# Stationary weight tiles of a hybrid decoder block: two K tiles laid out column by column in turn

## The chip, the cores and the metric

The kernel runs on one core of one Trainium2 chip. The metric is device time in microseconds (us) of one execution, as the median of several runs. A NeuronCore has five engines with instruction lists of their own: TensorE (PE in the profile; PEld is its loading of stationary weights, LDWEIGHTS), VectorE (DVE), ScalarE (ACT), GpSimd (POOL) and SyncE (SP, which here only issues DMAs). A matmul on TensorE holds a stationary block of 128 x 128 values in the array and streams a moving operand of up to 512 columns past it. Each matmul of this kernel has its own weight load.

## The reference, cut to what matters

One decoder layer over 256 tokens of width 2048, in fp32: a combined input projection, gated linear attention (GLA) and forgetting attention (FoX), a merge of the two with gates, an output projection and a layer norm, a gated MLP of width 5632 with a causal convolution on its gate path, a second layer norm, and a per-layer embedding. The parts that the change touches are plain matrix products of the token matrix with weights:

```python
proj = x @ w_in                                   # fq, fk, gq, gk are columns of it, 1024 each
...
g = causal_dwconv(x @ w_gate, conv_w, conv_b)     # x: (256, 2048), w_gate, w_up: (2048, 5632)
h = jax.nn.gelu(g) * (x @ w_up)
return h @ w_down
```

## The kernel before

Each fp32 matrix is split into a high part, rounded to the TensorE format fp32r, and a low part, the rest, and a product is built from high x high, high x low and low x high. A token tile holds, for one K tile of 128 rows, 256 columns of the high part of the activations and then 256 of the low part (`a[:, kt % 4, :]`, 512 columns).

The weights come from HBM as "units" of 128 partitions x 2048 fp32 values, 284 in all, in the order of use. `prep` fetches a unit as two halves of 1024 columns (`raw`), lets ScalarE round each into a tile `hi`, and VectorE subtract that into a tile `lo`; these tiles sit in rings of six. `unit()` hands out the next one and keeps three units ahead prepared. The order of the instructions on each engine follows the program and Tile's scheduler; SP issues its DMAs in program order.

Units are used in two ways. In most stages the activations are stationary and the weights stream past them (`x_mm`, `q_unit`: lines 353, 841, 979). In the stages that need their result with channels on partitions the weights are stationary: the FoX and GLA queries and keys (PSUM tiles psfq, psfk, psq, psk, 32 units) and the gate and up projections of the MLP (psg, psu, 88 units). There a unit is 128 output channels: 16 K tiles of 128 x 128 side by side, the first eight in `hi[0]` and `lo[0]`, the others in `hi[1]` and `lo[1]`. `w_unit` runs, for each K tile, one matmul of 512 columns with the block of `hi` (line 307) and one of 256 columns with the block of `lo` (line 309), all into one PSUM bank. `w_phase` does the same for the first three units of the MLP, in two phases by token half (lines 322 and 326, 256 columns each), while the layer norm before it still finishes. `comb` then adds the two halves of the bank. `_wst` lays the weights out on the host, before the launch.

Two other places are used for comparison in what follows: lines 713 to 718, in the GLA blocks, where levels 1 to 7 work on runs of 1, 2, 4 ... 64 words out of 2, 4, 8 ... 128; and plain fp32 matmuls (lines 628, 630, 735), which TensorE runs in two passes.

Of the kernel before, what the change touches and what calls it, by code (L numbers as in the profile page):

```python
# [19 lines left out]
P = 128  # L20
# [58 lines left out]
def tile_block(ctx: ExitStack, tc: tile.TileContext, wu, wfv, wpp, xT_in, x_in, pT_in, wlr,  # L79
               chan, gnorm, lng, ident_in, mask_in, cmask_in, out):  # L80
    nc = tc.nc
# [32 lines left out]
    def mmtile(name):  # L114
        return pmm.tile([P, 512], F32, tag="mm", name=name)
# [133 lines left out]
    def unit(ahead=3):  # L249
        u = n_used[0]  # L250
        n_used[0] += 1
        while n_prep[0] < min(NU, u + ahead):
            prep()
        return ready.pop(u)
# [42 lines left out]
            nc.gpsimd.tensor_copy(mask[:, 4 * i:4 * i + 4, :], maskf)  # L297


    def w_unit(ps, hi, lo, act, kts, first, last, hoff=0, tick=None):  # L300


        n = len(kts)
        for i, kt in enumerate(kts):
            a = act[kt // 4]
            w0 = (hoff + i) * P
            nc.tensor.matmul(ps, lhsT=hi[i // 8 if hoff == 0 else 0][:, w0 % 1024:w0 % 1024 + P],  # L307
                             rhs=a[:, kt % 4, :], start=first and i == 0, stop=False)
            nc.tensor.matmul(ps[:, 256:512],  # L309
                             lhsT=lo[i // 8 if hoff == 0 else 0][:, w0 % 1024:w0 % 1024 + P],  # L310
                             rhs=a[:, kt % 4, 0:256], start=False, stop=last and i == n - 1)
            if tick is not None:
                tick(i)

    def w_phase(ps, hi, lo, act, t, kts, part=slice(None)):


        p4 = ps.rearrange("p (s t n) -> p s t n", s=2, t=2)
        for kt in kts[part]:
            a = act[kt // 4][:, kt % 4, :]  # L320
            w = slice(kt % 8 * P, kt % 8 * P + P)
            nc.tensor.matmul(p4[:, :, t, :], lhsT=hi[kt // 8][:, w],
                             rhs=a.rearrange("p (s t n) -> p s t n", s=2, t=2)[:, :, t, :],
                             start=t == 0 and kt == kts[0], stop=False)
            if t == 1:
                nc.tensor.matmul(ps[:, 256:512], lhsT=lo[kt // 8][:, w], rhs=a[:, 0:256],
                                 start=False, stop=kt == kts[-1])

    def comb(ps, o, scale=1.0):
# [28 lines left out]
    def pull(n, gens=mixers):  # L358
        for _ in range(n):
            while gens:  # L360
                try:
                    next(gens[0])
                    break
                except StopIteration:
                    gens.pop(0)
# [92 lines left out]
    for u in range(8):  # L458
        hi, lo = fvu[u]
        for j in range(2):  # L460
            kt = 2 * u + j
            a = xT[kt // 4][:, kt % 4, :]
# [6 lines left out]
            for t, i, c in seq:  # L469
                o, n = fch[c]  # L470
                w, x = prods[t][i]
                nc.tensor.matmul(fbk[t][c][:, 0:n], lhsT=x, rhs=w[:, o:o + n],  # L472
                                 start=kt == 0 and i == 0, stop=kt == 15 and i == 2)
# [32 lines left out]
    for t in range(2):  # L506
        for c, (o, n) in enumerate(fch):
            n = min(n, 1024 - o)
# [143 lines left out]
    for n in range(16):  # L652
        h, j = n // 2, n % 2
        hi, lo = unit()

        ps = (mxtile if n == 0 else mmtile)(f"psf{'qk'[j]}{h}")
        w_unit(ps, hi, lo, xT, range(16), True, True,
               tick=lambda i: pull(1) if i == 7 else None)
        if n % 8 == 0:
            fqk[h // 4] = s8([P, 4, 2, 256], name=f"fqk{h // 4}")  # L660
        comb(ps, fqk[h // 4][:, h % 4, j], (P ** -0.5, 1.0)[j])
        if n >= 1:
            pull(1, parks)
# [105 lines left out]
    for n in range(16):  # L769
        nm, dst, sc = (("q", gq, 1.0 / 16.0), ("k", gk, 1.0))[n // 2 % 2]  # L770
        h, c = n // 4, n % 2
        hi, lo = unit()
        ps = mmtile(f"ps{nm}{2 * h + c}")
        w_unit(ps, hi, lo, xT, range(16), True, True,
               tick=lambda i: pull(1, mixers if n < 4 else levels) if i == 7 else None)
        comb(ps, dst[:, h, :].rearrange("p (t c n) -> p t c n", t=2, c=2)[:, :, c, :], sc)
        if n >= 4:
            pull(1)
        if n >= 1:
            pull(1, parks)  # L780
# [10 lines left out]
    def s_sums(y):  # L791

        a11, a21, a12, a22 = [y[:, k, t * P:t * P + P] for k in range(2) for t in range(2)]
        v = t2("sums").rearrange("p (i t) -> p i t", t=P)
        for i, a, b, op in ((0, a21, a22, ALU.add), (2, a21, a11, ALU.subtract),
                            (1, v[:, 0], a11, ALU.subtract), (3, a12, v[:, 1], ALU.subtract)):
            nc.vector.tensor_tensor(v[:, i], a, b, op)
        return v
# [328 lines left out]
    for n in range(PSM1, 32):  # L1127
        if n in (26, 28):
            i = n // 2 - 13
# [189 lines left out]
    pq, first = [], []  # L1319

    def end1(tail_mm):
# [4 lines left out]
        with tc.manual_schedule(engines={mybir.EngineType.PE}):  # L1326
# [16 lines left out]
            def phase0(i, part):  # L1343
                if i == len(us):
                    us.append(unit())
                    ps.append(mmtile(("psg0", "psu0", "psg1")[i]))
                w_phase(ps[i], *us[i], x1T, 0, kts, part)

            def phase1(j):
                for i in range(3):  # L1350
                    w_phase(ps[i], *us[i], x1T, 1, kts, slice(4 * j, 4 * j + 4))
# [60 lines left out]
    def gate_up(name):  # L1412
        if first:
            return first.pop(0)
        hi, lo = unit()
        ps = mmtile(name)
        w_unit(ps, hi, lo, x1T, range(16), True, True)
        return ps

    for n in range(NF):  # L1420
# [20 lines left out]
        pair, j = n // 2, n % 2  # L1441
# [12 lines left out]
        if pair in DN_S[0] and j == 1:  # L1454
            v = s_sums(yp)
            for i in range(2):
                w = sm.tile([P, 2, 256], F32R, tag="t2", bufs=6, name="hs")
# [3 lines left out]
                k = DN_S[0].index(pair)  # L1461
# [193 lines left out]
def _wst(w):  # L1655

    k, n = w.shape
    kt, nt = k // P, n // P
    per = 2048 // (kt * P)
    a = w.reshape(kt, P, nt // per, per, P).transpose(2, 1, 3, 0, 4)  # L1660
    return a.reshape(nt // per, P, 2048)


def _xst(w):
# [36 lines left out]
def _layout(i):  # L1701
    w_in = i["w_in"][0]
    c = lambda nm, n: w_in[:, OFF[nm]:OFF[nm] + n]
    bg, bf = _qst(i["w_branch_gla"][0]), _qst(i["w_branch_fox"][0])
    br = [w for q in range(4) for w in (bg[4 * q:4 * q + 4], bf[2 * q:2 * q + 2])]
    gu = np.stack([_wst(i["w_gate"][0]), _wst(i["w_up"][0])], 1).reshape(2 * NF, P, 2048)
    qk = np.stack([_wst(c(n, 1024)).reshape(4, 2, P, 2048) for n in ("gq", "gk")], 1)
    m = np.concatenate([_qst(c(n, 2048)) for n in ("ma", "mb")], 0)
    wu = np.concatenate(
        [np.stack([_wst(c("fq", 1024)), _wst(c("fk", 1024))], 1).reshape(16, P, 2048), qk.reshape(16, P, 2048), m[:PSM1],  # L1710
         _sst(c("gv", 2048), GV_ORDER, GV_S), _sst(c("gr", 2048), GV_ORDER, GR_S), m[PSM1:]] + br
        + [_sst(i["w_out"][0], OUT_ORDER, WO_S), gu,
# [45 lines left out]
```

## Time and profile before

| | |
|---|---|
| median of 3 runs | 1645.58 us (1645.08 to 1645.61) |
| span of the profiled execution, first to last instruction | 1645.0 us |
| TensorE matmuls, weight loads | 8422 each |
| busy: TensorE, weight loads, VectorE, ScalarE | 1638.4, 1404.3, 1356.0, 910.3 us |
| granted TensorE clock | 1.000 of full speed |
| read from HBM, written | 417.53 MB, 58.73 MB |

A row of the groups by line has the line, the engine, the operation, the tiles written and read, the shape and the count, then the busy time in us and the mean ns of one, then the idle time ahead of it and what ended it. A row of the timeline has the start in us, the duration in us, and the operation; "x2" at its end means that two like instructions in a row are merged, and the duration runs from the first's start to the last's end. Intervals of matmuls overlap, so the distance between two starts, not the duration, is what one matmul costs.

### The profile page before, as it was taken

To read this page: it belongs to the slowest core of one execution; us is meant where nothing else is said; L and a number is where in the kernel's file an instruction comes from. 1 tells how busy PE (TensorE), PEld (TensorE's weight loads), DVE (VectorE), ACT (ScalarE), POOL (GpSimd) and SP (SyncE) were. 2 spreads that over 40 slices of the span, in tenths; PEclk is the share of its full clock that TensorE was granted. 3 is DMA by queue.
4 is the path that set the end of the run, shared out by engine and by line. 5 is a ranking of instruction groups with operands and counts; after the bars stand their busy time and mean duration, and the time that the engine had idled before them with its cause. 6 is when DMAs were issued, how large, how long until landed. Compare 5 with 4: busy or idle time off the path is not lost.

```text
span 1645.0 us, 23490 instructions
## 1 busy us (share of the span) xinstructions
PE 1638.4 (100%) x8422; PEld 1404.3 (85%) x8422; DVE 1356.0 (82%) x1964; ACT 910.3 (55%) x1277; POOL 92.7 (6%) x244
## 2 busy tenths in 40 slices
PE   9999999999999999999999999999999999999998
PEld 9988888888888888887898888888888888888887
DVE  7687899788989867778987888887887778988887
ACT  6655555456666654446574445555455456566554
POOL 0000000000000000000010111110111000000000
PEclk9999999999999999999999999999999999999999
DMA  8799799878888768889855898888766679899574
GB/s 324 281 371 341 290 383 356 294 258 309 306 333 307 252 207 303 305 335 364 296 190 194 315 338 320 308 306 304 279 239 217 210 260 336 305 343 348 177 258 157
DMA packets 114838, 477.81 MB, mean 290 GB/s; under 512 B 13032, under 2 KB 14320, under 8 KB 95136
## 3 DMA queue, kind: packets, MB, share of 16 engines
q1 hardware_dynamic: 105216, 417.57, 70.8%
q0 software_dynamic: 9504, 58.73, 8.9%
q8 instruction: 66, 1.08, 0.2%
q14 instruction: 52, 0.43, 0.1%
HBM read 417.53 MB, written 58.73 MB: 290 GB/s over the span
## 4 chain that ended last, share of the span: by engine, by line
PE 97%; DMA 1%; DVE 1%; ACT 0%; issue 0%; POOL 0%; ACTq 0%
PE psm L979 11%; PE dn L841 10%; PE psu L307 10%; PE psg L307 9%; PE psa L979 5%; PE psu L309 5%; PE psg L309 5%; PE dn_p L841 4%; PE gr L841 3%; PE gv L841 3%; PE fv L472 3%; PE pg L353 3%; PE psb L979 3%; PE wo L841 2%; PE gr_p L841 2%; PE gv_p L841 2%
## 5 line engine op out<-in xcount | busy, mean ns | idle before, releaser
L241 DVE TENSOR_TENSOR lo<-raw,hi 128x1024 fp32r<-128x1024 f32 x456 | 551.1, 1220 | 140.7 <-ACT hi L121 139.4
L121 ACT ACTIVATE hi<-raw 128x1024 fp32r<-128x1024 f32 x456 | 476.6, 1057 | 304.2 <-DMA raw<-in_wu_dram 83.7
L307 PE MATMUL psu<-x1T,hi 128*128 128x512 f32 x688 | 240.4, 392 | 0.0
L307 PE MATMUL psg<-x1T,hi 128*128 128x512 f32 x672 | 234.8, 392 | 0.0
L309 PE MATMUL psu<-x1T,lo 128*128 128x256 f32 x688 | 192.3, 280 | 0.0
L309 PE MATMUL psg<-x1T,lo 128*128 128x256 f32 x672 | 187.8, 280 | 0.0
L979 PE MATMUL psm<-hi,xT 128*128 128x512 f32 x512 | 163.0, 392 | 0.0
L307 PEld LDWEIGHTS psu<-x1T,hi 128*128 128x128 f32 x688 | 129.2, 188 | 27.6
L307 PEld LDWEIGHTS psg<-x1T,hi 128*128 128x128 f32 x672 | 126.2, 188 | 27.0
L309 PEld LDWEIGHTS psu<-x1T,lo 128*128 128x128 f32 x688 | 130.6, 190 | 0.0
L121 ACT ACTIVATE hi_b<-raw 128x512 fp32r<-128x512 f32 x112 | 92.9, 841 | 66.8 <-DMA raw<-in_wu_dram 17.9
L309 PEld LDWEIGHTS psg<-x1T,lo 128*128 128x128 f32 x672 | 127.6, 190 | 0.0
L159 DVE TENSOR_TENSOR td<-td 128x512 f32<-128x512 f32 x172 | 117.6, 684 | 0.9
L215 DVE TENSOR_TENSOR lo_b<-raw,hi_b 128x512 fp32r<-128x512 f32 x112 | 104.9, 952 | 15.9 <-ACT hi_b L121 15.6
L979 PEld LDWEIGHTS psm<-hi,xT 128*128 128x128 f32 x512 | 96.2, 188 | 19.6
L215 DVE TENSOR_TENSOR lo_t<-td,hi_t 128x1024 fp32r<-128x1024 f32 x86 | 101.7, 1219 | 12.7 <-ACT hi_t L121 12.0
L121 ACT ACTIVATE hi_t<-td 128x1024 fp32r<-128x1024 f32 x86 | 88.0, 1053 | 28.9 <-DMA td<-td 15.1
L979 PE MATMUL psm<-lo,xT 128*128 128x512 f32 x256 | 99.8, 390 | 0.0
L841 PE MATMUL dn<-hi,hC 128*128 128x512 f32 x352 | 97.8, 389 | 0.0
L979 PE MATMUL psa<-hi,oT 128*128 128x512 f32 x256 | 81.2, 392 | 0.0
L841 PEld LDWEIGHTS dn<-hi,hC 128*128 128x128 f32 x352 | 66.0, 188 | 13.7
L979 PEld LDWEIGHTS psa<-hi,oT 128*128 128x128 f32 x256 | 48.1, 188 | 10.0
(414 smaller groups left out, 3130.8 us busy)
## 6 DMA issues: line engine op xcount, KB each, us to landing
raw<-in_wu_dram SPq DMA_DIRECT2D x525, 512.0 KB, 6.3
td<-in_wu_dram SPq DMA_DIRECT2D x43, 1024.0 KB, 8.8
td<-td POOLq DMA_DIRECT2D x43, 1024.0 KB, 7.7
td<-td SPq DMA_DIRECT2D x43, 1024.0 KB, 8.3
hS<-sd SPq DMA_DIRECT2D x11, 1024.0 KB, 8.8
raw<-in_wu_dram SPq DMA_DIRECT2D x43, 256.0 KB, 7.7
fvraw<-in_wfv_dram SPq DMA_DIRECT2D x13, 524.0 KB, 6.6
sd<-hs POOLq DMA_DIRECT2D x24, 256.0 KB, 5.6
```

The source lines that it names most:

```text
L121: return nc.scalar.activation(o, i, AF.Copy, bias=0.0, scale=scale)
L159: sub = lambda o, a, b: nc.vector.tensor_tensor(o, a, b, ALU.subtract)
L215: nc.vector.tensor_tensor(lo, src, hi.bitcast(F32), ALU.subtract)
L241: i = nc.vector.tensor_tensor(lo, raw, hi.bitcast(F32), ALU.subtract)
L307: nc.tensor.matmul(ps, lhsT=hi[i // 8 if hoff == 0 else 0][:, w0 % 1024:w0 % 1024 + P], rhs=a[:, kt % 4, :], start=first and i == 0, stop= ...
L309: nc.tensor.matmul(ps[:, 256:512], lhsT=lo[i // 8 if hoff == 0 else 0][:, w0 % 1024:w0 % 1024 + P], rhs=a[:, kt % 4, 0:256], start=False, ...
L353: nc.tensor.matmul(bs[j][:, 0:m], lhsT=x, rhs=v[:, o:o + m], start=first and i == 0, stop=last and i == 2)
L472: nc.tensor.matmul(fbk[t][c][:, 0:n], lhsT=x, rhs=w[:, o:o + n], start=kt == 0 and i == 0, stop=kt == 15 and i == 2)
L841: nc.tensor.matmul(ps[:, e], lhsT=x, rhs=w, start=k == 1, stop=k == total.get(id(ps), 3 * ns))
L979: nc.tensor.matmul(ps[t], lhsT=x, rhs=v, start=first and i == 0 and j == 0, stop=last and i == 3 and j == 2)
```

## The change

`_wst` interleaves pairs of K tiles: where column n of K tile 2m stood beside column n + 1 of the same tile, it now stands beside column n of K tile 2m + 1. A unit keeps its size and its place; a half of 1024 columns still holds eight K tiles, now as four pairs of 256 columns. The new function `wcols` takes the block of one K tile out of that: 128 columns with a step of two elements (8 bytes), spread over 1024 bytes, where it was 128 columns side by side. `w_unit` and `w_phase` read their stationary blocks through it, `hi` and `lo` alike. The parameter `hoff`, which no caller set, is gone. The moving operands, the PSUM tiles, the DMAs, the rounding and the subtraction stay as they are. The lists of instructions on TensorE, VectorE, ScalarE, GpSimd and SP are the same before and after, row for row.

```diff
+    def wcols(w, kt):
+
+        v = w[kt // 8].rearrange("p (k n j) -> p k j n", n=P, j=2)
+        return v[:, kt % 8 // 2, kt % 2, :]
+
-    def w_unit(ps, hi, lo, act, kts, first, last, hoff=0, tick=None):
+    def w_unit(ps, hi, lo, act, kts, first, last, tick=None):
...
-            w0 = (hoff + i) * P
-            nc.tensor.matmul(ps, lhsT=hi[i // 8 if hoff == 0 else 0][:, w0 % 1024:w0 % 1024 + P],
-                             rhs=a[:, kt % 4, :], start=first and i == 0, stop=False)
-            nc.tensor.matmul(ps[:, 256:512],
-                             lhsT=lo[i // 8 if hoff == 0 else 0][:, w0 % 1024:w0 % 1024 + P],
-                             rhs=a[:, kt % 4, 0:256], start=False, stop=last and i == n - 1)
+            nc.tensor.matmul(ps, lhsT=wcols(hi, i), rhs=a[:, kt % 4, :],
+                             start=first and i == 0, stop=False)
+            nc.tensor.matmul(ps[:, 256:512], lhsT=wcols(lo, i), rhs=a[:, kt % 4, 0:256],
+                             start=False, stop=last and i == n - 1)
...
-            w = slice(kt % 8 * P, kt % 8 * P + P)
-            nc.tensor.matmul(p4[:, :, t, :], lhsT=hi[kt // 8][:, w],
+            nc.tensor.matmul(p4[:, :, t, :], lhsT=wcols(hi, kt),
...
-                nc.tensor.matmul(ps[:, 256:512], lhsT=lo[kt // 8][:, w], rhs=a[:, 0:256],
+                nc.tensor.matmul(ps[:, 256:512], lhsT=wcols(lo, kt), rhs=a[:, 0:256],
...
 def _wst(w):
...
-    kt, nt = k // P, n // P
-    per = 2048 // (kt * P)
-    a = w.reshape(kt, P, nt // per, per, P).transpose(2, 1, 3, 0, 4)
-    return a.reshape(nt // per, P, 2048)
+    a = w.reshape(k // 256, 2, P, n // P, P).transpose(3, 2, 0, 4, 1)
+    return a.reshape(n // P, P, k)
```

## The prediction

> **What bounds the kernel now.** I read the page first: the busy times, the granted clock and the chain of work that ended last.
>
> ```profile
> span 1645.0 us, 23490 instructions
> PE 1638.4 (100%) x8422; PEld 1404.3 (85%) x8422; DVE 1356.0 (82%) x1964; ACT 910.3 (55%) x1277; POOL 92.7 (6%) x244
> PEclk9999999999999999999999999999999999999999
> PE 97%; DMA 1%; DVE 1%; ACT 0%; issue 0%; POOL 0%; ACTq 0%
> ```
>
> TensorE carries 97% of the chain at full granted clock in every slice. A busy TensorE is not a proof, since its intervals overlap, so I asked the view of waits for everything that TensorE waited for.
>
> ```profile
> PE warm_ps L131 <- DVE warm L128: 1.2, 1, 1.2
> PE wo L841 <- DVE lo_b L215: 0.4, 1, 0.4
> PE wo_p L841 <- ACT hi_t L121: 0.2, 1, 0.2
> ```
>
> That is 1.8 us in all. The time is therefore the sum of the steps from the start of one matmul to the start of the next, and a nanosecond more or less in a step is paid once per step. The profiled span of 1645.0 us lies 0.6 us under the median of the runs, 1645.58, whose spread is 0.5 us; I work on the span and give the result as if it were the median. About 0.2% (3.3 us) is what a measurement of this kernel can tell from no change.
>
> **Which steps the edit touches.** The groups by line give the number of matmuls whose stationary block is a weight tile, that is all of `w_unit` (lines 307 and 309) and `w_phase` (322 and 326).
>
> ```profile
> L309 PE MATMUL psu<-x1T,lo 128*128 128x256 f32 x688 | 192.3, 280 | 0.0
> L309 PE MATMUL psg<-x1T,lo 128*128 128x256 f32 x672 | 187.8, 280 | 0.0
> L309 PE MATMUL psfq<-xT,lo 128*128 128x256 f32 x128 | 35.9, 280 | 0.0
> L309 PE MATMUL psk<-xT,lo 128*128 128x256 f32 x128 | 35.8, 280 | 0.0
> L309 PE MATMUL psfk<-xT,lo 128*128 128x256 f32 x128 | 35.8, 280 | 0.0
> L309 PE MATMUL psq<-xT,lo 128*128 128x256 f32 x128 | 35.8, 280 | 0.0
> L322 PE MATMUL psg<-x1T,hi 128*128 128x256 f32 x64 | 12.6, 287 | 0.0
> L322 PE MATMUL psu<-x1T,hi 128*128 128x256 f32 x32 | 6.3, 284 | 0.0
> L326 PE MATMUL psg<-x1T,lo 128*128 128x256 f32 x32 | 7.9, 282 | 0.0
> L326 PE MATMUL psu<-x1T,lo 128*128 128x256 f32 x16 | 4.0, 282 | 0.0
> ```
>
> Line 309 runs 688 + 672 + 4 x 128 = 1872 times, and line 307 as often, since the loop issues one of each per K tile. Lines 322 and 326 add 144. So 3888 of the 8422 weight loads change their access pattern. 1872 matmuls are 512 wide; 1872 + 144 = 2016 are 256 wide. The timeline shows how the two widths alternate inside one unit:
>
> ```profile
> 899.74 0.39 PE L307 MATMUL psg<-x1T,hi 128*128 128x512 f32 x1
> 899.97 0.28 PE L309 MATMUL psg<-x1T,lo 128*128 128x256 f32 x1
> 900.09 0.39 PE L307 MATMUL psg<-x1T,hi 128*128 128x512 f32 x1
> ...
> 904.59 0.39 PE L307 MATMUL psg<-x1T,hi 128*128 128x512 f32 x1
> 899.97 0.19 PEld L307 LDWEIGHTS psg<-x1T,hi 128*128 128x128 f32 x1
> ```
>
> Fourteen pairs lie between 899.74 and 904.59: 4.85 / 14 = 0.3464 us a pair. The wide matmul takes 0.23 us of that, the narrow one 0.116. The last row is the point of the whole case: the weights of the next wide matmul begin to load at 899.97, when the narrow one starts, and have only its 0.116 us to hide behind.
>
> **How much room the load has.** The load's 0.19 us is a latency; its pace shows where loads follow each other.
>
> ```profile
> 209.11 0.97 PEld L735 LDWEIGHTS pa<-kq 128*128 128x128 f32 x8
> L1223 PEld LDWEIGHTS ptl<-ident,z 128*128 128x128 f32 x64 | 7.7, 140 | 1.9 <-ACT z L1216 0.5
> L307 PEld LDWEIGHTS psu<-x1T,hi 128*128 128x128 f32 x688 | 129.2, 188 | 27.6
> ```
>
> Eight loads of 128 contiguous fp32 columns take 0.97 us, so (0.97 - 0.19) / 7 = 0.111 us each. These have a 128-wide matmul each over them, so 0.111 is an upper bound of the load's own time. Against the 0.116 us of the narrow step that leaves 5 ns of cover, and against the 0.23 us of the wide step about 120 ns. The second row, the load for a transpose (mean 140 ns), takes 48 ns less than the third, a load of the edited line: the reading side can deliver the same 512 bytes faster than the usual load asks for them.
>
> **The change part by part.** No instruction is added, removed or moved; the two loops over weight tiles issue the same matmuls, with the same operands' tiles, in the same order. DMA sizes, ScalarE's rounding and VectorE's subtraction still run over whole contiguous 1024-column tiles, so they cost what they did. Unchanged terms: 0. What changes is that a load reads 128 words 8 bytes apart, over 1024 bytes, where it read 512 bytes in a run. No load of before does that, so I bound its price by other engines that read every second fp32 word. In level 1 of the GLA blocks (lines 713 to 718) ScalarE and VectorE work on 256 words with step two; in the later levels the same lines work on runs.
>
> ```profile
> 186.93 0.44 ACT L713 ACTIVATE e<-e 128x256 f32<-128x256 f32 x1 [2.33 <-DVE e L710]
> 187.26 0.43 ACT L715 ACTIVATE e<-e 128x256 f32<-128x256 f32 x1
> 194.26 0.41 ACT L713 ACTIVATE e<-e 128x256 f32<-128x256 f32 x1
> 194.57 0.41 ACT L715 ACTIVATE e<-e 128x256 f32<-128x256 f32 x1
> L718 DVE TENSOR_TENSOR kq<-gk,e x28: 408/416/426, 188.0 to 365.3; 128x256 f32<-128x256 f32 x28
> ```
>
> ScalarE takes 0.435 us at step two (first two rows, level 1 of head 0) against 0.41 at runs of 32 (level 6): 25 ns for 256 words, 0.1 ns a word. VectorE's 28 products over all seven levels lie within 408 to 426 ns: no surcharge. For a load of 128 words that makes 0 (VectorE's row) to 13 ns (ScalarE's). I take ScalarE's, because the load's pace, 128 words in at most 0.111 us, is nearer to ScalarE's than to VectorE's. The load then takes 111 + 13 = 124 ns. Under a wide matmul that stays hidden. Under a narrow one it sticks out by 124 - 116 = 8 ns, 2016 times: **16 us**. Sum: 1645.6 + 16 = **1661.6 us**.
>
> The two ends of this term. Below: if the load is at VectorE's price it stays covered, 0 us. Above: the reading could also hold up the moving stream. How much of that there is now can be bounded by plain fp32 matmuls, which take their moving columns at half the pace:
>
> ```profile
> 153.21 0.59 PE L628 MATMUL po<-pts,fv 128*128 128x256 f32 x2
> 153.64 0.38 PE L630 MATMUL po<-pts,fv 128*128 128x128 f32 x2
> ```
>
> Two passes over 256 columns start 0.43 us before the next line, 0.215 each, so half of that, 0.1075, is what 256 columns would take with nothing in the way. A pair has 768 columns: 0.3225 us against 0.3464 measured, 24 ns of surplus. If all of it came from loads crossing the moving stream, and twice the span read doubled it, the price would be 1872 x 24 ns = 45 us: 1691. It can also go the other way, below.
>
> [...]
>
> **The rivals.**
>
> *It costs nothing.* The 5 ns of cover are enough, or the load's own time lies well under 111 ns. For it: VectorE's row and the transposes' faster load. Against it: ScalarE's rows, and that the narrow step has so little room. Time: 1645.6, within 3.3 us.
>
> *It makes the steps shorter (the other sign).* Now the load advances at half the byte rate of the moving operand, so the two streams pass each other; with step two a load of 1024 bytes runs beside 256 moving words, 1024 bytes, at nearly equal pace. If the 24 ns of surplus come from the streams crossing, running in step could remove them in every pair. All of it would be 45 us, 1600; half, which I take as the price, 1623. It decides from 1.8 ns a pair (3.3 us / 1872). For it: the surplus exists, and the two streams do run side by side. Against it: nothing in the trace shows that the surplus comes from loads. What is late next would not be another engine soon:
>
> ```profile
> 900.00:1380.00 480.00, 480.00 (x2691) 421.11 (x2690) 387.10 (x602) 249.22 (x366) 50.10 (x151) 1.00 0.79 284
> ```
>
> In this stretch of the gate and up units VectorE (the third busy time) works 387 of 480 us; with 7% taken off the pairs it would be at 87%.
>
> *The load falls to half its pace.* If single words can't be read at the pace of runs, the load takes 222 ns: just hidden under the wide step, 106 ns too long under the narrow one, 2016 x 106 = 214 us: 1860. For it: no load in this trace reads with a step. Against it: neither ScalarE nor VectorE loses more than 6% at this step. [...]
>
> **How the numbers follow.** Forecast, slower by the surcharge, 1649 to 1691: 0.35, because an extra line read is likely to cost something where cover is 5 ns. Half pace: 0.16. Together slower by over 0.2%: 0.51. Nothing: 0.21. Shorter steps: 0.28. The likeliest gives 1661.6. The range leaves out half pace (0.16) and the last few us of the shorter steps: 1604 to 1691, which holds the forecast's bounds, the case of nothing and nearly all of the gain. Cases of both signs hold most of the chance; the forecast's own range is 1649 to 1691.
>
> **What would show it.** Right: the groups of lines 307 and 309 keep their counts, the loads of line 307 read some 13 ns longer than their 188, the wide step stays 0.23 and the narrow one grows from 0.116 to about 0.124, so that fourteen pairs take 4.96 us; the waits of TensorE stay near 1.8 us. Nothing: pairs stay at 0.346. Shorter steps: pairs fall toward 0.33 and both widths lose. Half pace: the narrow step is near 0.22 and the loads near 0.3. The forecast is wrong if the pair moves in its wide half, if steps of lines that are not edited (841, 979) move, or if TensorE begins to wait for weights.

## The result and the profile after

| | before | after |
|---|---|---|
| median | 1645.33 us (1644.32 to 1645.61, 4 runs) | 1657.12 us (1656.67 to 1657.49, 4 runs) |
| span of the profiled execution | 1645.0 us | 1655.2 us |

The changed kernel takes 1.0071 times as long, 95% interval 1.0056 to 1.0085: +11.8 us, 9.2 to 14.0 by the interval. The forecast was 1661.6, +16. Lines shift by two to four in the changed file: 307 and 309 are 311 and 313, 841 and 979 are 843 and 981. In the three kernels below that edit one kind of load only, 307 and 309 are 315 and 317. The page after, and its waits of TensorE:

```profile
span 1655.2 us, 23490 instructions
PE 1649.3 (100%) x8422; PEld 1419.6 (86%) x8422; DVE 1357.1 (82%) x1964; ACT 909.7 (55%) x1277; POOL 93.8 (6%) x244
PE 99%; DVE 0%; ACT 0%; POOL 0%; issue 0%; ACTq 0%
PE warm_ps L131 <- DVE warm L128: 1.2, 1, 1.2
```

Counts are as they were, VectorE and ScalarE work as long as before, TensorE waits for no other engine after the warm-up. The loss has to be inside the steps of TensorE. The groups of the page, for one of the tiles:

```profile
L311 PE MATMUL psu<-x1T,hi 128*128 128x512 f32 x688 | 245.0, 398 | 0.0
L313 PE MATMUL psu<-x1T,lo 128*128 128x256 f32 x688 | 191.3, 278 | 0.0
L981 PE MATMUL psm<-hi,xT 128*128 128x512 f32 x512 | 163.0, 392 | 0.0
L311 PEld LDWEIGHTS psu<-x1T,hi 128*128 128x128 f32 x688 | 135.5, 197 | 26.7
L313 PEld LDWEIGHTS psu<-x1T,lo 128*128 128x128 f32 x688 | 136.0, 198 | 0.0
```

Edited loads take 197 and 198 ns where they took 188 and 190. The wide matmul shows 398 where it showed 392, the narrow one 278 where it showed 280, and line 981, whose stationary operand is not edited, its 392 as before. One unit in the timeline, from its first wide matmul to that of the next unit:

```profile
1104.98 0.40 PE L311 MATMUL psg<-x1T,hi 128*128 128x512 f32 x1
1105.21 0.28 PE L313 MATMUL psg<-x1T,lo 128*128 128x256 f32 x1
...
1110.63 0.40 PE L311 MATMUL psu<-x1T,hi 128*128 128x512 f32 x1
```

Sixteen pairs in 5.65 us: 0.3531 a pair, against 0.3464 in the rows of before. Over the whole trace I summed the distances between starts: from a wide to the next narrow matmul 432.3 us before and 444.8 after (1872 of each), from a narrow one on 219.4 and 218.7, all others 987.4 and 985.8. So +12.5 - 0.7 - 1.6 = +10.2 us, the difference of the spans. The mean pair went from 0.3467 to 0.3531 us, 6.4 ns. This mean and those of pairs and steps below leave out the few steps, 10 to 20 of 3744 in each trace, that are over 1.2 times as long as the middle one of their kind.

One thing contradicts the prediction at first sight: the growth stands in the wide step, 0.2296 to 0.2364 us, not in the narrow one, which stays at 0.117.

### The profile page after: what moved, and what is told of

The parts are those of the page before. It is cut to its first block, busy times and chain, and to the rows that moved or that the text cites. A ratio compares the mean times of both kernels' runs of the same rounds, so it can differ in the third digit from the quotient of the medians.

```text
span 1655.2 us, 23490 instructions
## 1 busy us (share of the span) xinstructions
PE 1649.3 (100%) x8422; PEld 1419.6 (86%) x8422; DVE 1357.1 (82%) x1964; ACT 909.7 (55%) x1277; POOL 93.8 (6%) x244
## 4 chain that ended last, share of the span: by engine, by line
PE 99%; DVE 0%; ACT 0%; POOL 0%; issue 0%; ACTq 0%
PE psm L981 11%; PE dn L843 10%; PE psu L311 10%; PE psg L311 10%; PE psa L981 5%; PE psu L313 5%; PE psg L313 5%; PE dn_p L843 4%; PE wo L843 3%; PE gr L843 3%; PE gv L843 3%; PE fv L474 3%; PE pg L355 3%; PE psb L981 3%; PE gr_p L843 2%; PE psq L311 2%
## 5 line engine op out<-in xcount | busy, mean ns | idle before, releaser
L311 PE MATMUL psu<-x1T,hi 128*128 128x512 f32 x688 | 245.0, 398 | 0.0
L311 PE MATMUL psg<-x1T,hi 128*128 128x512 f32 x672 | 239.3, 398 | 0.0
L311 PEld LDWEIGHTS psu<-x1T,hi 128*128 128x128 f32 x688 | 135.5, 197 | 26.7
L311 PEld LDWEIGHTS psg<-x1T,hi 128*128 128x128 f32 x672 | 132.4, 197 | 26.2
L313 PEld LDWEIGHTS psu<-x1T,lo 128*128 128x128 f32 x688 | 136.0, 198 | 0.0
L313 PEld LDWEIGHTS psg<-x1T,lo 128*128 128x128 f32 x672 | 132.8, 198 | 0.0
```

The costliest lines, as they stand in the source:

```text
L311: nc.tensor.matmul(ps, lhsT=wcols(hi, i), rhs=a[:, kt % 4, :], start=first and i == 0, stop=False)
L313: nc.tensor.matmul(ps[:, 256:512], lhsT=wcols(lo, i), rhs=a[:, kt % 4, 0:256], start=False, stop=last and i == n - 1)
```

## Which of the two loads costs

The lo blocks load beside a wide matmul, the hi blocks beside a narrow one. Two kernels take the edit for one kind only.

```diff
 # hi only
-            nc.tensor.matmul(ps[:, 256:512], lhsT=wcols(lo, i), rhs=a[:, kt % 4, 0:256],
+            nc.tensor.matmul(ps[:, 256:512], lhsT=wone(lo, i), rhs=a[:, kt % 4, 0:256],
 # lo only
-            nc.tensor.matmul(ps, lhsT=wcols(hi, i), rhs=a[:, kt % 4, :],
+            nc.tensor.matmul(ps, lhsT=wone(hi, i), rhs=a[:, kt % 4, :],
 # both
+    def wone(w, kt):
+        return w[kt // 8][:, kt % 8 * P:kt % 8 * P + P]
```

> Only the blocks of hi, which load beside the narrow matmul, are read with step two; the blocks of lo are read as 128 columns side by side out of the interleaved tile, so the low product has other columns than the reference. Theory 1, as predicted (the strided load takes 8 to 9 ns longer and sticks out of the narrow step): nearly all of the loss stays, +10 to +13 us over before, a pair takes 0.353 us and the loads of lo are back at 0.188 to 0.190. Theory 2 (a strided load holds up the stream of the matmul that it runs beside, most of all the full-length wide one): no loss, within 3 us of before, the wide step back from 0.2366 to 0.2296. Theory 3 (both loads count alike): +6 us, a pair of 0.350.

> Only the blocks of lo, which load beside the wide matmul with about 120 ns of cover, are read with step two; the blocks of hi are read side by side out of the interleaved tile, so the high products have other columns than the reference. Theory 1 (the load sticks out of the narrow step): no loss, within 3 us of before, pair 0.3467. Theory 2 (the load holds up the stream that it runs beside): nearly all of the loss, +10 to +13 us, wide step 0.2366. Theory 3 (both alike): +6 us, pair 0.350.

Hi only: 1657.15 us, ratio 1.0074 (1.0057 to 1.0091), the whole loss. Lo only: 1647.18 us, 1.0012 (1.0002 to 1.0022), with runs spread from 1644.9 to 1650.9, and a mean pair of 0.3469 in its trace, 0.2 ns over before. The trace is of a run of 1645.79 us; the longest five of the ten runs, from 1648.3 us on, have none. The groups of hi only (first four rows) and lo only:

```profile
L315 PE MATMUL psu<-x1T,hi 128*128 128x512 f32 x688 | 245.0, 399 | 0.0
L317 PE MATMUL psu<-x1T,lo 128*128 128x256 f32 x688 | 192.7, 280 | 0.0
L315 PEld LDWEIGHTS psu<-x1T,hi 128*128 128x128 f32 x688 | 135.1, 196 | 30.9
L317 PEld LDWEIGHTS psu<-x1T,lo 128*128 128x128 f32 x688 | 130.7, 190 | 0.0
```

```profile
L315 PE MATMUL psu<-x1T,hi 128*128 128x512 f32 x688 | 240.5, 392 | 0.0
L317 PE MATMUL psu<-x1T,lo 128*128 128x256 f32 x688 | 193.5, 281 | 0.0
L315 PEld LDWEIGHTS psu<-x1T,hi 128*128 128x128 f32 x688 | 129.2, 188 | 24.1
L317 PEld LDWEIGHTS psu<-x1T,lo 128*128 128x128 f32 x688 | 133.6, 194 | 0.0
```

The loads of lo take longer in the second kernel (194) and next to nothing follows from it. The loads of hi, with the narrow matmul beside them, carry the loss; and the group that grows is that of the matmul which needs those weights. Theory 2, that a strided load slows the stream beside it, the wide one above all, would have had it the other way round. If the wide matmul is recorded as started while it still waits for its weights, a late load lengthens the wide step. The next experiment shows such a wait at a size that can't be mistaken; whether the 6 to 7 ns of the changed kernel are one is a question for the end.

## What sets the load's own time

> Four K tiles are laid out column by column in turn, so each block is read with a step of four elements, one word out of each 16 bytes; it computes the reference. If the price goes with the bytes spanned (128 spans of 16 bytes where step two has 64 and step one 32), the surcharge of a pair triples from 6.7 to 20 ns: +37 us, 1683. If step two was the last step at which the load nearly keeps its pace and single words per 16 bytes halve it, the narrow step goes to 0.22 and the time to about 1850. If the price is per step that is not one, whatever its size, it stays at +12 us.

> Blocks of 128 words with a step of three elements, starting 80 columns apart in the tile as it was; the blocks are not those of the K tiles, only the reading pattern counts. The first experiments leave one theory: a load that outlasts the narrow matmul beside it makes the next wide one wait for its weights. What sets the load's own time is open. Theory A (16-byte lines): from step two to step four, 64 to 128 lines, the loads of the all-narrow phases go from 0.1207 to 0.234 us, 1.77 ns a line; step three touches 96 lines, 0.177 us, so a pair of about 0.410 and 1772 us in all. Theory B (two words in a line are enough, one is not, and then every word costs a line): step three falls to nearly the pace of step four, a pair of 0.45 to 0.467, 1855 to 1890 us.

```diff
 # step four (and four K tiles interleaved on the host)
+        v = w[kt // 8].rearrange("p (k n j) -> p k j n", n=P, j=4)
+        return v[:, kt % 8 // 4, kt % 4, :]
 # step three (the reading pattern alone)
+        o = kt % 8 * 80
+        return w[kt // 8][:, o:o + 3 * P - 2:3]
```

Step four: 1887.34 us, ratio 1.1473 (1.1456 to 1.149). Step three: 1773.98 us, 1.078 (1.0749 to 1.0811). A unit of each, step four first:

```profile
1105.41 0.51 PE L311 MATMUL psu<-x1T,hi 128*128 128x512 f32 x1
1105.75 0.28 PE L313 MATMUL psu<-x1T,lo 128*128 128x256 f32 x1
...
1112.88 0.51 PE L311 MATMUL psg<-x1T,hi 128*128 128x512 f32 x1
```

```profile
1105.81 0.46 PE L311 MATMUL psg<-x1T,hi 128*128 128x512 f32 x1
1106.10 0.28 PE L313 MATMUL psg<-x1T,lo 128*128 128x256 f32 x1
...
1112.39 0.46 PE L311 MATMUL psu<-x1T,hi 128*128 128x512 f32 x1
```

At step four the wide matmul shows 0.51 us, the step to the narrow one is 0.34 and the narrow step still 0.12: the wait, some 115 ns, is booked on the wide step. Pairs are 0.467 and 0.411 us.

To see the load by itself I took the cover away: the narrow matmul cut to 128 columns, at step two and at step one.

```diff
-            nc.tensor.matmul(ps[:, 256:512], ..., rhs=a[:, kt % 4, 0:256], ...
+            nc.tensor.matmul(ps[:, 256:384], ..., rhs=a[:, kt % 4, 0:128], ...
```

> The changed kernel with the narrow matmul of w_unit cut to 128 columns, so that half of the low product is left out; nothing but the load of the next block of hi can then set the narrow step. If the load at step two binds already: the pair stays near 0.353 us. If the surcharge were a cost of the matmul's own, the pair falls by about half of the narrow step, to 0.30.

> The kernel before with the narrow matmul of w_unit cut to 128 columns (half of the low product left out). If the contiguous load takes its upper bound of 0.111 us, the pair falls from 0.3467 to about 0.344, and the difference to the run with step two is the load's surcharge, 8 to 10 ns. If the contiguous load is much faster than that, the pair falls further, down to 0.30, and the surcharge is larger than the 6.7 ns that the changed kernel shows.

The times of one execution each are 1655.89 us (step two) and 1635.57 (step one). Step two first, then step one:

```profile
1103.74 0.45 PE L311 MATMUL psg<-x1T,hi 128*128 128x512 f32 x1
1104.03 0.22 PE L313 MATMUL psg<-x1T,lo 128*128 128x128 f32 x1
...
1109.37 0.45 PE L311 MATMUL psu<-x1T,hi 128*128 128x512 f32 x1
```

```profile
1102.08 0.44 PE L307 MATMUL psg<-x1T,hi 128*128 128x512 f32 x1
1102.36 0.22 PE L309 MATMUL psg<-x1T,lo 128*128 128x128 f32 x1
...
1107.52 0.44 PE L307 MATMUL psu<-x1T,hi 128*128 128x512 f32 x1
```

These sixteen pairs give 0.352 and 0.340; the means over the trace are 0.3515 and 0.3404. Half of the narrow matmul is gone, and the step-two pair hardly moves (0.3531 to 0.3515). Less the 0.2296 of the wide step of before, a load takes 0.122 us at step two and 0.111 at step one, 11 ns apart. That supposes that the wide step itself is as before in the step-two kernel, which the last run of this document puts in doubt.

A late load shows in one more place, the start of the load after it. The load of lo starts 3 ns after the wide matmul in the kernel before, and 51 (step one) and 61 ns (step two) after it in the two kernels with 128 columns; at step four it is 95 ns. In the changed kernel it is 3 ns, as before. The sign may miss a few ns: the lo-only kernel of the next section, whose wide step grew by 4 ns, shows no later start either. Step four, 128 columns at step two, and the changed kernel; their wide matmuls, shown above, start at 1105.41, 1103.74 and 1104.98:

```profile
1105.50 0.33 PEld L313 LDWEIGHTS psu<-x1T,lo 128*128 128x128 f32 x1
1103.80 0.20 PEld L313 LDWEIGHTS psg<-x1T,lo 128*128 128x128 f32 x1
1104.98 0.20 PEld L313 LDWEIGHTS psg<-x1T,lo 128*128 128x128 f32 x1
```

The subtraction gives 0.182 us for step three (mean pair 0.4117). At step four (0.4675) it would give 0.238, but there a load is longer than the wide step's 0.2296 too, so the pair should be two loads, 0.234 each. The phases need no subtraction, since every load there stands beside a matmul of 256 columns: their median step is 0.118, 0.120, 0.175 and 0.234 us at steps one to four. At steps three and four that is 1.82 and 1.83 ns per 16 bytes of span that the block covers (96 and 128 of them). Theory A of the step-three run holds: a load of 0.177 and 1772 us were expected, 0.175 and 1773.98 measured. At 1.83 ns, the 64 spans of step two would take 0.117 us, an estimate under the 0.122 of the subtraction. At step one there are 32 spans, 59 ns at that rate, and the load takes 0.111 all the same, 0.87 ns a word. So by that estimate step two, 0.117 us against the 0.111 of step one, is just past the point where the span, not the number of words, sets the time.

## What cover does

> Step four for the blocks of lo alone, which load beside a wide matmul, four K tiles interleaved; the blocks of hi are read side by side out of that tile and are not the reference's. Step four takes 0.234 us a load in the all-narrow phases; the wide step before was 0.2296. If only what sticks out counts: the pair rises by 0 to 8 ns, 0 to 15 us, and the 48 lo loads of the phases add 6 us: 1651 to 1666. If a load at step four costs its 120 ns wherever it stands: +225 us.

This is the lo-only kernel with four K tiles interleaved. It took 1662.94 us, ratio 1.0105 (1.0076 to 1.0135).

```profile
L315 PE MATMUL psu<-x1T,hi 128*128 128x512 f32 x688 | 244.9, 396 | 0.0
L317 PEld LDWEIGHTS psu<-x1T,lo 128*128 128x128 f32 x688 | 212.6, 309 | 0.0
```

A load at step four shows 119 ns more than the 190 of before, and beside a wide matmul 17 us is all that comes of it instead of 225; 5 of the 17 are in the phases. The mean pair is 0.3533, its wide step 0.2337 instead of 0.2296, which is about what a load of 0.234 would make of it.

The last question on cover: every load beside a wide matmul, by streaming the low product 512 columns wide.

```diff
-            nc.tensor.matmul(ps[:, 256:512], lhsT=..., rhs=a[:, kt % 4, 0:256],
+            nc.tensor.matmul(ps, lhsT=..., rhs=a[:, kt % 4, :],
```

> The changed kernel with the low product of w_unit streamed 512 columns wide (low times low added, a product that the reference's precision does not need), so that every strided load has a wide matmul beside it. The extra columns cost about 0.110 us a pair, 206 us, here and in the run with step one. If only what sticks out of the neighbour counts, this run and the one with step one have the same time within 3 us and the same pair, 0.455 to 0.460 us; if every strided load costs something of its own, this one is 6 to 12 us longer.

> The kernel before with the low product of w_unit streamed 512 columns wide; the partner of the run with step two. About 1645 + 206 = 1851 us, a pair of 0.455 to 0.460 us.

Step two 1858.39 us (1856.59 to 1858.47), step one 1866.65 (1866.15 to 1867.19). Step two first:

```profile
1103.91 0.39 PE L311 MATMUL psg<-x1T,hi 128*128 128x512 f32 x1
1104.14 0.39 PE L313 MATMUL psg<-x1T,lo 128*128 128x512 f32 x1
...
1111.27 0.39 PE L311 MATMUL psu<-x1T,hi 128*128 128x512 f32 x1
```

```profile
1100.71 0.40 PE L307 MATMUL psu<-x1T,hi 128*128 128x512 f32 x1
1100.94 0.40 PE L309 MATMUL psu<-x1T,lo 128*128 128x512 f32 x1
...
1108.15 0.40 PE L307 MATMUL psg<-x1T,hi 128*128 128x512 f32 x1
```

With cover everywhere step two costs nothing more, and neither expectation of this pair holds: step two is 8.3 us the shorter one. Its pairs are 0.460 and nearly all its steps 230 ns; with step one the steps wander between 226 and 239. Something other than the load's length is at work.

## What is not the load's length

> The kernel before, with the blocks of lo in w_unit cut to 64 columns for all K tiles but the last, so that the load beside each wide matmul reads half as much; half of the low-weight product is left out. It asks where the 24 ns a pair above the half pace of plain fp32 come from. If from loads that cross the moving stream: the wide step falls by 5 to 8 ns, the time by 9 to 15 us. If the moving stream has them of its own: wide step 0.2296 as before, time within 3 us, only the loads of lo shorter.

```diff
+            m = P if i == n - 1 else 64
-            nc.tensor.matmul(ps[:, 256:512], lhsT=<block of lo>, rhs=a[:, kt % 4, 0:256],
+            nc.tensor.matmul(ps[:m, 256:512], lhsT=<block of lo>[:, 0:m], rhs=a[:, kt % 4, 0:256],
```

1645.37 us, ratio 0.9999 (0.999 to 1.0009).

```profile
L307 PE MATMUL psu<-x1T,hi 128*128 128x512 f32 x688 | 240.4, 392 | 0.0
L310 PEld LDWEIGHTS psu<-x1T,lo 128*64 128x64 f32 x645 | 87.7, 136 | 0.0
```

Half the load (136 ns for 190) leaves the wide matmul at its 392. So the surplus of the wide step, 0.2296 us over the 0.215 that the prediction's estimate from the passes of plain fp32 makes for 512 columns, isn't paid per word loaded beside it. The exact half in that estimate was not shown: 256 columns take 0.215 us in a plain fp32 pass and 0.117 in the narrow step.

> The kernel before with LO_SHIFT = 0: the lo tiles of the edited stages start 64 bytes lower, so their blocks begin at a multiple of 128 bytes like those of hi. If loads and moving stream meet in the memory, the pair depends on where the block starts: 0.340 to 0.353 instead of 0.3467, 5 to 12 us either way. If not: within 3 us.

Only the number `LO_SHIFT` changes, 16 to 0. 1655.03 us, ratio 1.006 (1.0043 to 1.0076): 9.4 us lost with every load at step one and none of them longer in the mean than 188 to 189 ns.

```profile
1102.86 0.40 PE L307 MATMUL psg<-x1T,hi 128*128 128x512 f32 x1
1103.09 0.28 PE L309 MATMUL psg<-x1T,lo 128*128 128x256 f32 x1
...
1108.51 0.40 PE L307 MATMUL psu<-x1T,hi 128*128 128x512 f32 x1
```

Pairs of 0.353 here, 0.3519 in the mean, of which the wide step has 0.2353 and the narrow one 0.1165; the changed kernel has 0.2364 and 0.1167. Where a block starts, by 64 bytes, costs four fifths of what the whole edit did, and in the same place. That asks whether the edit's loss is of this kind after all, so the last run gave the changed kernel's narrow matmul 64 columns more, cover enough for a load of 0.122.

> The changed kernel with the narrow matmul of w_unit 64 columns wider (320, written 64 columns lower in the bank, so its result is not the reference's). With 64 columns at 0.4375 ns (from 256 to 512 columns the step grows by 112 ns) the narrow step is about 0.145 us, longer than the load's 0.122. If the loss is the load sticking out and nothing else, it is covered now: pair 0.3467 + 0.028 = 0.3747 us, about 1698 us. If part of the 6.4 ns has another cause, such as where the strided block lies, the pair stays above that, up to 0.381 and 1710 us.

```diff
-            nc.tensor.matmul(ps[:, 256:512], lhsT=wcols(lo, i), rhs=a[:, kt % 4, 0:256],
+            nc.tensor.matmul(ps[:, 192:512], lhsT=wcols(lo, i), rhs=a[:, kt % 4, 0:320],
```

1707.96 us, ratio 1.0378 (1.036 to 1.0395).

```profile
1103.07 0.40 PE L311 MATMUL psg<-x1T,hi 128*128 128x512 f32 x1
1103.31 0.31 PE L313 MATMUL psg<-x1T,lo 128*128 128x320 f32 x1
...
1109.15 0.40 PE L311 MATMUL psu<-x1T,hi 128*128 128x512 f32 x1
```

The pair is 0.380, 5 ns above the 0.3747 of the load theory alone: the narrow step takes 0.1458, longer than any of the figures for the load, and the wide step 0.2342 all the same, 4.6 ns over before. So "sticks out and nothing else" is refuted at this width: with the load covered, the steps of this kernel are still not the best ones. No run at step one with 320 columns was made, so it is open whether the 5 ns belong to step two or to that width; nor was the changed kernel run with another `LO_SHIFT`.

## What was right in the prediction and what was not, point by point

**The bound.** Right: the time is the sum of TensorE's steps, and nothing outside them moved by more than 2 us.

**The place.** Right as to the loads: those of hi, beside the narrow matmul, carry the loss (hi only +11.8 us, lo only +1.8 with a nearly unchanged pair in its trace), and loads beside a wide one have room, up to the 17 us of step four.

**The price of the load.** ScalarE's rows gave 13 ns. The pairs with 128 columns give 11, the rate of steps three and four 6, and the load's own record grew by 9 (188 to 197 ns). The bound from its own pace, 0.111 us, was the pace itself. VectorE's row, no surcharge, would have been the wrong row to take. No run shows the extra line read that the chance of 0.35 leans on; what they show is the rate of steps three and four, 1.82 and 1.83 ns per 16 bytes of span.

**What sticks out.** 8 ns were predicted, 124 less 116. The runs bound this term and don't settle it. At most it is 121.9 less 117.1, 4.8 ns, if the wide step in the kernel with 128 columns at step two is the 0.2296 of before. If that step is the 0.2342 of the run with 320 columns, the load is 0.117 and next to nothing sticks out; the estimate of 0.117 from steps three and four says the same, and the load of lo, which starts as early as before, shows no wait either, though that sign may miss a few ns. The pair lost 6.4 ns. So between 1.6 and all of them are a longer wide step that is no wait for late weights. The prediction's sum had no such term; it named a moving stream held up by the reading only for the upper end of its range. What causes it is open: `LO_SHIFT` 0 lengthens the same step by 5.7 ns with every load at step one, while with 512 columns beside every load step two has none of it. That +12 us came out near +16 is therefore luck in part, and possibly in the main: a smaller stick-out, or none, and an addend that was not in the sum.

**The count.** 2016 steps were charged; the 1872 pairs pay, while the 144 steps of the phases took 0.1 us more in all, where 1.2 were charged.

**How it would show.** Wrong. The prediction said that the narrow step would grow to 0.124 and that a growth in the wide half would refute the forecast. It did grow there, 0.2296 to 0.2364. At steps three and four the wait for late weights is booked on the wide step (0.46 and 0.51 us in the rows, for 0.39 before), so the sign could not tell the forecast's wait from a slower wide stream; by it the forecast's mechanism is neither refuted nor confirmed.

**The rivals.** "It costs nothing" fails by 11.8 us, though its argument, that the 5 ns of cover are enough, may have held: step two cost a load 6 to 11 ns over its 111, while at steps three and four a load takes 0.175 to 0.182 and 0.234 us. So half pace, 0.222 us by the prediction, came at step four, not at step two. "Shorter steps" did not come in this kernel; its doubt was sound that the surplus comes from loads (half the load beside the wide matmul changed nothing), but with every load covered step two was 8.3 us ahead, and with `LO_SHIFT` 0 a start moved by 64 bytes cost 9.4. That the two streams meet there is a guess; no run shows it.

## What to carry to other kernels

In these runs a weight load was nearly free only as long as the matmul beside it streamed: at step four, 0.234 us a load, the loads of lo, beside wide steps of 0.2296 us and in the phases, cost 17 us, and those of hi and lo together 242. So ask of each kind of load which neighbour covers it, and price an edit of the load at the narrowest neighbour, not at all of them. When the trace shows a matmul growing, look one load back before blaming the matmul, since the wait for its weights stood in its own time here (0.51 us for 0.39 at step four); then look whether the next load starts late (95 ns after the wide matmul for 3), and make a run with the load covered, before calling a few ns a wait. Of the steps one to four, step two, two fp32 words per 16 bytes, was the widest at which a block still loaded at nearly the pace of a run (0.117 to 0.122 us for 0.111).

## What the runs showed of the hardware that I had not expected

At steps three and four a load of 128 fp32 words took 1.82 and 1.83 ns per 16 bytes of span (0.175 and 0.234 us in the phases); at step one it took 0.111 us, 0.87 ns a word, and at step two between 0.117 (an estimate from that rate) and 0.122. Moving the lo blocks by 64 bytes, with nothing else in the program changed, moved the kernel by 9.4 us (ratio 1.006, 1.0043 to 1.0076). And with 512 columns beside every load the steps were an even 230 ns at step two, and between 226 and 239 at step one.
